# Values of two dilated-attention sections: strided tokens in the matmul, or natural order and a round trip through DRAM

## The chip, the cores and the metric

The program runs on one core of one Trainium2 chip, in one launch. The metric is the device time of that core in microseconds (us). A core has a matrix engine (TensorE, "PE" in the profile, with its weight loads apart as "PEld"), three engines for elementwise work (VectorE "DVE", ScalarE "ACT", GpSimd "POOL"), and queues that issue DMAs (SP, ACT and POOL here). Each engine takes its instructions in the order in which the program lists them.

## What is computed

The reference is a two-layer network of one kind (a convolution with a recurrence, then differential attention) followed by a two-layer network of another. Only the second matters here: each of its two layers mixes tokens by four attentions and then applies a mixture of experts. One of the four is a dilated attention with three branches, each of four heads of width 64:

```python
DIL_BRANCHES = ((128, 1), (512, 4), (2048, 16))
...
q = br(_rope(flat(q), pos))
k = br(_rope(flat(k), pos))
v = br(v)
...
idx = qpos[:, None] - dil * jnp.arange(n_keys)[None, :]
kb = jnp.take(k, idx, axis=1)
vb = jnp.take(v, idx, axis=1)
z = jnp.einsum('bqhd,bqnhd->bhqn', qb, kb) * scale
outs.append(jnp.einsum('bhqn,bqnhd->bhqd', (p / den), vb))
```

There are 512 tokens. In the branches with dilation 4 and 16 a token attends only to tokens of its own residue modulo 4. So the kernel sorts the tokens of these two branches into four classes of 128 tokens (class r holds tokens r, r+4, r+8, ...), and attends within a class.

## The kernel before

Precision is float32, made of pieces: every operand is split into a high part (ACT, L214) and a low part (DVE, L215), and `mm3` (L260 to L265) multiplies three pairs of parts, so three matmuls stand for one. The profile shows them as lines L263, L264 and L265.

Each layer's `mixing` (L1026) runs *sections*. A section projects all tokens to queries and keys (four "columns" j = 0 to 3 of 512 tokens each) and then to values: `value(i, k)` for four groups i of 128 tokens and eight slices k of the input, which is 4 x 8 x 3 = 96 matmuls of 128x256 per section. In a value matmul the tokens `xT` are the stationary operand, the one that a weight load (PEld) puts into the array before each matmul; in a column they are the moving one.

Sections s1 (dilation 4) and s2 (dilation 16) have `classes=True`. Their value matmuls take the tokens of class i at once, by the slice `slice(i, T, 4)` (L1145): every fourth float32 of a row of `xT`. The values land in PSUM in class order and ACT copies them into `r.v` (L1150), a tile with 64 values and a constant 1.0 per head. The queries and keys of these sections are sorted in another way: `rope2` (L1164) computes them in natural order and the split into parts writes them in class order.

`dilated` (L1243) builds the attention of a section: `scores` (L1264; masks L1271, products L1193, row maximum on DVE L1199, exponent on ACT L1204), `transposed` (L1211, copied by ACT L1213), `values` (L1277; products with `r.v`, L1280) and a copy of the result (ACT L1256). `weave` interleaves two lists of steps by their listed costs: d1, the attention of s1, with the columns and values of s2; then d2, the attention of s2, with section s0; then d0 with sb. The values of s1 are not interleaved with anything. The order on PE is fixed by these lists; on the other engines a scheduler sets it when the program is built.

Other parts that the prediction's steps touch:

- `rope2` of column j: ACT and DVE shift halves (L1170, L1171), POOL multiplies by the sine (L1172), DVE multiplies by the cosine (L1173) and adds (L1174), then ACT and DVE split (L214, L215, tile `qd`). L1173 is the last that reads the column's PSUM bank.
- Columns and values share two PSUM banks called `mm` in turn (in s2: columns 0 and 2 and the first pair of value groups use one, columns 1 and 3 and the second pair the other), so a column or a pair of value groups can start only when the `rope2` of the second-last user has read its bank.
- `done` (L998) splits the next weight chunk (tile `wpart`) once the old one has been read, half a chunk at a time.
- `gain` (L481) scales the residual stream (`x`, L486 and L487, on DVE here) and `lend_x` (L1099) copies it to DRAM from the POOL queue (L1103), which lends its tiles to the pool of buffers that `grab` hands out.
- `natural` (L1324) is a round trip through DRAM that exists already: it writes the result of d1 or d2 to DRAM in 128 runs of 4,224 bytes (L1328) and reads it back in token order in 512 runs of 1,056 bytes (L1331), both issued from POOL.

Of the kernel before, what the change touches and what calls it, by code (L numbers as in the profile page):

```python
# [13 lines left out]
F32 = mybir.dt.float32  # L14
# [3 lines left out]
AF = mybir.ActivationFunctionType  # L18
# [5 lines left out]
P = 128  # L24
T = 512
# [104 lines left out]
class _Net:  # L130
# [981 lines left out]
    def section(self, xT, ids, buf, rope=False, classes=False, first=None):  # L1112


        nc = self.nc
        r = SimpleNamespace(steps=[])
        ps = {}

        def column(j, k, toks):
            self.pump()  # L1120
            if (j, k) == (0, 0) and toks.start == 0:
                r.qk = [self.quad_tile(buf, n, [2, T], F32R) for n in range(4)]
            if k == 0 and toks.start == 0:
                ps[j] = self.ps("s" if first and j > 1 else "mm")
            w, o = self.chunk(ids[j // 2]), j % 2 * P
            self.mm3(ps[j][:, toks], [t[:, k, o:o + P] for t in w], [t[:, k, toks] for t in xT], k == 0, k == KD - 1)
            if k < KD - 1 or toks.stop < T:
                return
            if j % 2:
                self.done(ids[j // 2])  # L1130
            parts = r.qk[j][:, 0], r.qk[j][:, 1]
            if rope:
                self.rope2(ps[j], parts, classes, 0.125 if j < 2 else 1.0)
            elif j < 2:
                self.split_scaled(*parts, ps[j], 0.125)
            else:
                self.split(*parts, ps[j])

        def value(i, k):
            self.pump()  # L1140
            if (i, k) == (0, 0):
                r.v = self.vs.pop(0)
            if i % 2 == 0 and k == 0:
                ps["v"] = self.ps("mm")
            toks = slice(i, T, 4) if classes else slice(i * P, (i + 1) * P)  # L1145
            o = i % 2 * 256
            self.mm3(ps["v"][:, o:o + 256], [t[:, k, toks] for t in xT], [t[:, k] for t in self.chunk(ids[2])],
                     k == 0, k == KD - 1)
            if k == KD - 1 and i % 2:
                nc.scalar.activation(r.v[:, i - 1:i + 1, :, 0:64],  # L1150
                                     ps["v"].rearrange("p (i h d) -> p i h d", i=2, h=4), AF.Copy)
                if i == NT - 1:
                    self.done(ids[2])

        for toks in [slice(0, 256), slice(256, T)] if first else [slice(0, T)]:
            for j in range(4):
                if first and toks.start == 0 and 1 <= j <= 2:
                    r.steps.append((0.8, first[j - 1]))
                r.steps += [(0.65, partial(column, j, k, toks)) for k in range(KD)]
        for i in range(NT):  # L1160
            r.steps += [(0.33, partial(value, i, k)) for k in range(KD)]
        return r
# [1121 lines left out]
```

## Time and profile before

| what | value |
|---|---|
| runs (median, lowest to highest) | 2792.08 us, 2788.1 to 2795.29, 3 runs |
| profiled execution: time | 2788.31 us |
| profiled execution: span of the profile | 2786.5 us |
| PE busy | 2664.2 us, 96% of the span |
| PE weight loads | 2232.6 us, 80% |
| DVE, ACT, POOL busy | 60%, 47%, 17% |
| mean granted clock of TensorE | 0.981 of full speed |

A busy PE means that some matmul was in flight; matmuls overlap, so how dense the stream is shows only in the distance between starts. The page gives shares over the whole program; what one stage costs is read from the timeline and the table of stretches.

### The profile page before, as it was taken

How to read it: one execution, taken by the hardware profiler on the slowest of the kernel's cores; microseconds unless marked ns; L12 is line 12 of the kernel's file. 1: busy time of each engine (PE TensorE's matmuls, PEld its weight loads, DVE VectorE, ACT ScalarE, POOL GpSimd, SP SyncE). 2: the span in 40 equal slices, each digit the busy share in tenths (PEclk: the TensorE clock that was granted, in tenths of full speed). 3: DMA queues.
4: the chain of work that ended last, by engine and by line, in shares of the span. 5: the costliest groups of instructions: out<-in, count | busy, mean ns of one | idle time of the engine just before them, and what ended most of it. 6: DMA issues, size and time to landing. Idle time of an engine off the chain costs nothing. (4 is left out here: it accounts for less than half of the span.)

```text
span 2786.5 us, 41347 instructions
## 1 busy us (share of the span) xinstructions
PE 2664.2 (96%) x14504; PEld 2232.6 (80%) x14508; DVE 1678.5 (60%) x2621; ACT 1315.5 (47%) x2076; POOL 469.4 (17%) x430
## 2 busy tenths in 40 slices
PE   8999999999999999999999969999899999799996
PEld 6768888887678888898887768888798877688885
DVE  7785323376866333374445587669764454856897
ACT  5643222255644222244564436558644554246784
POOL 2324000010104000011021141211111120411113
PEclk9999999999999999999999979999999999899998
DMA  6114323213104232322202049979422130279994
GB/s 224 51 46 166 106 84 106 91 71 113 46 31 166 91 98 91 106 78 105 83 31 104 18 178 290 305 220 354 170 91 98 35 111 23 106 256 283 352 366 181
DMA packets 93275, 385.05 MB, mean 138 GB/s; under 512 B 14688, under 2 KB 16480, under 8 KB 76768
## 3 DMA queue, kind: packets, MB, share of 16 engines
q1 hardware_dynamic: 76592, 329.14, 33.3%
q0 software_dynamic: 13408, 47.32, 6.3%
q10 hardware_dynamic: 3024, 5.56, 0.6%
q8 instruction: 118, 1.93, 0.3%
q14 instruction: 133, 1.09, 0.1%
HBM read 349.22 MB, written 32.77 MB: 137 GB/s over the span
## 5 line engine op out<-in xcount | busy, mean ns | idle before, releaser
L215 DVE TENSOR_TENSOR wpart<-raw,wpart 128x1024 fp32r<-128x1024 f32 (+3 forms) x385 | 525.6, 1395 | 315.1 <-ACT wpart L214 298.9
L214 ACT ACTIVATE wpart<-raw 128x1024 fp32r<-128x1024 f32 (+3 forms) x393 | 445.0, 1169 | 363.9 <-PE mm L264 180.5
L263 PE MATMUL mm<-xT,wpart 128*128 128x512 f32 (+1 forms) x1136 | 440.9, 388 | 16.1 <-ACT wpart L214 8.8
L264 PE MATMUL mm<-xT,wpart 128*128 128x512 f32 (+1 forms) x1136 | 428.5, 377 | 1.8 <-DVE xT L215 1.8
L265 PE MATMUL mm<-xT,wpart 128*128 128x512 f32 (+1 forms) x1136 | 427.9, 377 | 0.5 <-DVE wpart L215 0.5
L263 PEld LDWEIGHTS mm<-xT,wpart 128*128 128x128 f32 x1136 | 214.9, 189 | 57.8 <-ACT wpart L214 8.8
L263 PE MATMUL mm<-wpart,xT 128*128 128x256 f32 (+2 forms) x672 | 255.6, 380 | 0.0
L265 PEld LDWEIGHTS mm<-xT,wpart 128*128 128x128 f32 x1136 | 214.8, 189 | 44.3 <-DVE wpart L215 1.0
L264 PEld LDWEIGHTS mm<-xT,wpart 128*128 128x128 f32 x1136 | 215.2, 189 | 41.8 <-DVE xT L215 2.8
L265 PE MATMUL mm<-wpart,xT 128*128 128x256 f32 (+2 forms) x672 | 241.0, 359 | 0.3 <-DVE xT L215 0.2
L264 PE MATMUL mm<-wpart,xT 128*128 128x256 f32 (+2 forms) x672 | 240.2, 357 | 0.0
L349 POOL TENSOR_TENSOR sm<-sm,mhalf 128x4 f32<-128x4 f32 (+2 forms) x74 | 65.4, 884 | 1015.5 <-DVE sm L360 765.6
L264 PE MATMUL mm<-wpart,gT 128*128 128x256 f32 (+1 forms) x544 | 183.7, 338 | 0.0
L265 PE MATMUL mm<-wpart,gT 128*128 128x256 f32 (+1 forms) x544 | 183.2, 337 | 0.0
L263 PE MATMUL mm<-wpart,gT 128*128 128x256 f32 (+1 forms) x544 | 183.1, 337 | 0.0
L263 PEld LDWEIGHTS mm<-wpart,xT 128*128 128x128 f32 x672 | 144.7, 215 | 18.1 <-issue 5.0
L265 PEld LDWEIGHTS mm<-wpart,xT 128*128 128x128 f32 x672 | 144.6, 215 | 14.0 <-DVE xT L930 1.0
L264 PEld LDWEIGHTS mm<-wpart,xT 128*128 128x128 f32 x672 | 145.2, 216 | 10.0 <-issue 1.2
L562 DVE TENSOR_TENSOR silu<-silu,mm 128x512 f32<-128x512 f32 x44 | 30.2, 686 | 200.9 <-PE mm L265 200.9
L215 DVE TENSOR_TENSOR xT<-raw,xT 128x1024 fp32r<-128x1024 f32 x108 | 129.8, 1221 | 17.1 <-ACT xT L214 16.7
L263 PE MATMUL mm<-xT,hT 128*128 128x512 f32 x272 | 114.0, 419 | 1.6 <-ACT xT L214 1.6
L214 ACT ACTIVATE xT<-raw 128x1024 fp32r<-128x1024 f32 x108 | 111.0, 1052 | 5.0 <-DMA raw<-in_w_dram 4.9
(579 smaller groups left out, 5661.0 us busy)
## 6 DMA issues: line engine op xcount, KB each, us to landing
raw<-in_w_dram SPq DMA_DIRECT2D x324, 512.0 KB
raw<-in_gu_dram SPq DMA_DIRECT2D x40, 1024.0 KB
raw<-in_w_in_dram SPq DMA_DIRECT2D x30, 1024.0 KB
raw<-in_down_dram SPq DMA_DIRECT2D x16, 1024.0 KB
raw<-in_o_qk_dram SPq DMA_DIRECT2D x8, 1024.0 KB
raw<-in_w_out_dram SPq DMA_DIRECT2D x8, 1024.0 KB
raw<-in_e_in_dram SPq DMA_DIRECT2D x7, 1024.0 KB
raw<-in_down_dram SPq DMA_DIRECT2D x8, 768.0 KB
```

Of the source, the lines that this page charges most:

```text
L214: ins = self.nc.scalar.activation(hi, x, AF.Copy)
L215: self.last_lo = (eng or self.nc.vector).tensor_sub(lo, x, hi)
L263: mm(out, lhsT=ls[0], rhs=rs[0], start=start, stop=False)
L264: mm(out, lhsT=ls[0], rhs=rs[1], start=False, stop=False)
L265: mm(out, lhsT=ls[1], rhs=rs[0], start=False, stop=stop)
L349: self.last_rsqrt = self.nc.gpsimd.tensor_tensor(v, v, self.half[:, :n], op=ALU.pow)
L562: nc.vector.tensor_mul(s, s, ps[2 * j + 1])
```

## The change

In sections with `classes=True` the value matmuls take the tokens in natural order, 128 neighbours at a time, as the other sections do. Since the values then lie by token and not by class, they go through DRAM: ACT copies a pair of value groups (128x512) into a buffer, POOL's queue writes it to a DRAM tile `vperm` of 512 x 256 floats, and after the second pair a third DMA reads `vperm` back into `r.v`, partition j from tokens 4j to 4j+3, as 2,048 runs of 256 bytes (a head's 64 values; the constant beside them stays). Per section that adds two DMAs of 256 KB out and one of 512 KB in, all on POOL's queue, and two buffers; the ACT copy stays, with another destination. There are four such sections, s1 and s2 in each of two layers.

```diff
             if (i, k) == (0, 0):
                 r.v = self.vs.pop(0)
+                if classes:
+                    r.vd = self.dram.tile([T, 256], F32, name=self.uid("vperm"))
             if i % 2 == 0 and k == 0:
                 ps["v"] = self.ps("mm")
-            toks = slice(i, T, 4) if classes else slice(i * P, (i + 1) * P)
+            toks = slice(i * P, (i + 1) * P)
...
             if k == KD - 1 and i % 2:
-                nc.scalar.activation(r.v[:, i - 1:i + 1, :, 0:64],
-                                     ps["v"].rearrange("p (i h d) -> p i h d", i=2, h=4), AF.Copy)
+                if classes:
+
+                    v = self.grab()
+                    nc.scalar.activation(v, ps["v"], AF.Copy)
+                    nc.gpsimd.dma_start(r.vd[(i - 1) * P:(i + 1) * P].rearrange("(i p) c -> p i c", i=2),
+                                        v.rearrange("p (i c) -> p i c", i=2))
+                    self.drop(v)
+                else:
+                    nc.scalar.activation(r.v[:, i - 1:i + 1, :, 0:64],
+                                         ps["v"].rearrange("p (i h d) -> p i h d", i=2, h=4), AF.Copy)
                 if i == NT - 1:
                     self.done(ids[2])
+                    if classes:
+                        nc.gpsimd.dma_start(r.v[:, :, :, 0:64], r.vd.rearrange("(j r) (h d) -> j r h d", r=4, h=4))
```

Lines behind the change move by 12, so L1172 of before is L1184 of after, L1103 stays.

POOL in the first of the two layers, around the values of s1: `xk` are the copies of the residual stream x to DRAM, the multiplications are those of `rope2`. Before:

```order
L1172 TENSOR_TENSOR mx_8296<-mx_8296,cf 128x512
L1172 TENSOR_TENSOR mx_8298<-mx_8298,cf 128x512
L1103 DMA xk_8733<-x_76 128x1024
L1103 DMA xk_8733<-x_77 128x1024
L1172 TENSOR_TENSOR mx_8302<-mx_8302,cf 128x512
```

And after:

```order
L1184 TENSOR_TENSOR mx_8298<-mx_8298,cf 128x512
L1156 DMA vperm_8620<-mx_8300 128x2x256
L1156 DMA vperm_8620<-mx_8301 128x2x256
L1103 DMA xk_8737<-x_76 128x1024
L1165 DMA mx_8307<-vperm_8620 128x16x64
L1103 DMA xk_8737<-x_77 128x1024
L1184 TENSOR_TENSOR mx_8293<-mx_8293,cf 128x512
```

The read back (L1165) stands behind the third copy of x, and before the fourth and the first `rope2` of s2.

POOL in the same layer, around the values of s2, where `perm` is the round trip of d1's result. Before:

```order
L1172 TENSOR_TENSOR x_76<-x_76,cf 128x512
L1328 DMA perm_9119<-mx_8303 128x1056
L1331 DMA mx_8304<-perm_9119 128x4x264
L1172 TENSOR_TENSOR mx_8296<-mx_8296,cf 128x512
L1172 TENSOR_TENSOR x_76<-x_76,cf 128x512
```

And after:

```order
L1184 TENSOR_TENSOR x_76<-x_76,cf 128x512
L1156 DMA vperm_8995<-mx_8294 128x2x256
L1340 DMA perm_9127<-mx_8303 128x1056
L1156 DMA vperm_8995<-mx_8302 128x2x256
L1343 DMA mx_8304<-perm_9127 128x4x264
L1165 DMA mx_8308<-vperm_8995 128x16x64
L1184 TENSOR_TENSOR mx_8292<-mx_8292,cf 128x512
```

The two round trips are interleaved, and the read of the values stands behind both reads' waits, ahead of the first `rope2` of s0.

ACT keeps its order: the copy of a pair stands where L1150 stood. Around the values of s1 it is, after:

```order
L1182 ACTIVATE mx_8298<-s_8456 32x512
L1155 ACTIVATE mx_8300<-mm_8621 128x512
L214 ACTIVATE qd_8330<-mx_8297 128x128x4
L214 ACTIVATE qd_8331<-mx_8299 128x128x4
L214 ACTIVATE wpart_87<-raw_82 128x1024
L1155 ACTIVATE mx_8301<-mm_8675 128x512
L214 ACTIVATE wpart_87<-raw_82 128x1024
```

Here `qd_8330` and `qd_8331` are the splits of columns 2 and 3 and `wpart_87` the next chunk for the values of s2; nothing moved. On PE, DVE and ACT no instruction changes its place among the others anywhere in the mixing. On SP one load of output weights (L996) and two small loads (L1490) trade places later in the mixing. Since each of the four sections takes two more buffers from `grab`, the buffers that later steps get are others than before.

## Rows read from the trace of the kernel before

**Rows 1.** The page, part 1: busy time and share of each engine.
```profile
PE 2664.2 (96%) x14504; PEld 2232.6 (80%) x14508; DVE 1678.5 (60%) x2621; ACT 1315.5 (47%) x2076; POOL 469.4 (17%) x430
```

**Rows 2.** Stretches: start:end, length, us busy of PE, PEld, DVE, ACT, POOL, clock, DMA.
```profile
1236.00:1258.60 22.60, 22.60 (x100) 22.56 (x100) 19.90 (x22) 8.29 (x10) 4.97 (x4) 1.00 0.33 116
1258.60:1313.00 54.40, 54.40 (x294) 48.69 (x294) 26.38 (x32) 24.80 (x44) 6.38 (x7) 1.00 0.23 78
1313.00:1356.40 43.40, 43.35 (x293) 37.57 (x294) 22.98 (x31) 22.67 (x45) 6.46 (x6) 1.00 0.25 85
...
2041.40:2095.80 54.40, 54.40 (x293) 48.69 (x292) 25.84 (x32) 24.80 (x44) 5.84 (x6) 1.00 0.23 84
```

**Rows 3.** Groups by shape: weight loads of s1's values (strided tokens), 1236.0 to 1258.6.
```profile
L264 PEld LDWEIGHTS mm<-wpart,xT 128*128 128x128 f32 x32 | 10.6, 330 | 0.0
```

**Rows 4.** The same view for s0's values (neighbouring tokens), 1341.6 to 1356.4.
```profile
L264 PEld LDWEIGHTS mm<-wpart,xT 128*128 128x128 f32 x32 | 6.0, 188 | 0.0
```

**Rows 5.** Timeline, PE: start, duration, engine, line; s1's first value, d1's steps, s2's values.
```profile
1236.17 0.40 PE L263 MATMUL mm<-wpart,xT 128*128 128x256 f32 x1
...
1258.58 0.61 PE L1271 MATMUL s<-cb,identb 128*128 128x512 bf16 x2
1259.11 1.55 PE L1193 MATMUL s<-qd,qd 64*128 64x128 f32 x24
...
1268.40 0.60 PE L1211 MATMUL t<-cf,mx 128*128 128x128 f32 x4
...
1279.81 1.00 PE L1280 MATMUL o<-mx,mx 128*128 128x65 f32 x8
...
1281.40 0.39 PE L263 MATMUL mm<-xT,wpart 128*128 128x512 f32 x1
...
1287.35 0.48 PE L263 MATMUL mm<-wpart,xT 128*128 128x256 f32 x1
```

**Rows 6.** Timeline, PE, s0's values: two starts, 15 matmuls apart.
```profile
1342.08 0.28 PE L265 MATMUL mm<-wpart,xT 128*128 128x256 f32 x1
...
1343.84 0.28 PE L265 MATMUL mm<-wpart,xT 128*128 128x256 f32 x1
```

**Rows 7.** Timeline, DVE, s1's values to s2's first column; idle before, its releaser in brackets.
```profile
1249.22 1.08 DVE L215 TENSOR_TENSOR qd<-mx,qd 128x512 fp32r<-128x512 f32 x1 [0.75 <-ACT qd L214]
...
1257.06 1.23 DVE L215 TENSOR_TENSOR wpart<-raw,wpart 128x1024 fp32r<-128x1024 f32 x1 [1.60 <-ACT wpart L214]
...
1260.35 1.23 DVE L215 TENSOR_TENSOR wpart<-raw,wpart 128x1024 fp32r<-128x1024 f32 x1 [0.93 <-ACT wpart L214]
1261.49 1.28 DVE L1199 TENSOR_REDUCE sm<-s 128x4 f32<-128x512 f32 x2
1267.12 0.68 DVE L1171 TENSOR_SCALAR mx<-mm 32x512 f32<-32x512 f32 x1 [4.35 <-ACT mx L1170]
```

**Rows 8.** Timeline, ACT, same stretch: copy of the first pair, d1's first exponents.
```profile
1247.57 0.60 ACT L1150 ACTIVATE mx<-mm 128x512 f32<-128x512 f32 x1 [4.38 <-PE mm L265]
...
1262.21 2.17 ACT L1204 ACTIVATE mx<-s,sm 128x128 f32<-128x128 f32 x8 [1.90 <-DVE sm L1199]
```

**Rows 9.** Timeline, DVE: last read of the PSUM banks of s2's columns 1, 2, 3.
```profile
1279.98 0.69 DVE L1173 SCALAR_TENSOR_TENSOR mx<-mm,cf 128x512 f32<-128x512 f32 x1
1286.48 0.69 DVE L1173 SCALAR_TENSOR_TENSOR x<-mm,cf 128x512 f32<-128x512 f32 x1
1294.43 0.69 DVE L1173 SCALAR_TENSOR_TENSOR x<-mm,cf 128x512 f32<-128x512 f32 x1
```

**Rows 10.** Line L1328, the write of `natural`: time from issue to landing.
```profile
DMA to landing us min/median/max: 3.0/3.0/3.0
```

**Rows 11.** Line L1331, the read of `natural`: its issue, and its time to landing.
```profile
L1331 POOL DMA_DIRECT2D mx<-perm x4: 766/779/793, 1312.9 to 2141.0; - x4
...
DMA to landing us min/median/max: 4.1/4.1/4.1
```

**Rows 12.** The page, part 3: packets, MB and share of 16 engines of POOL's queue.
```profile
q0 software_dynamic: 13408, 47.32, 6.3%
```

## Prediction
> **What bounds the kernel now.** I read the page first: PE is busy for 96% of the span and its weight loads for 80%, while POOL, which gets the added work, has 17% [rows 1]. Then I read the stretch that the change touches, as a table of stages [rows 2]: in s1's values, in d1 with s2 and in d2 with s0, PE is busy nearly all the time at the full granted clock (1.00, the 2.4 GHz level). So a microsecond taken out of the matmul stream there is a microsecond of the program, unless another engine is late once PE is faster. The table has a hint of what can be taken out: d1 with s2 and d2 with s0 run the same steps with the same number of matmuls (294 and 293), but the first takes 54.40 us and the second 43.40 us, and weight loads are busy for 48.69 and 37.57 us. The one difference on PE is that s2 takes strided tokens in its values and s0 neighbours.
>
> The groups by shape confirm it. A weight load of the same shape from the same tile takes 330 ns with every fourth token [rows 3] and 188 ns with neighbours [rows 4]. What counts is the distance between starts: s1's 96 value matmuls run from 1236.17 to the start of d1 at 1258.58 [rows 5], 22.41 us or 233.4 ns each; s0's are 1.76 us for 15, or 117.3 ns each [rows 6].
>
> **The gain on PE.** Per section 96 x (233.4 - 117.3) ns = 11.1 us, the same as the 11.0 us between the two stages. The second layer repeats it (54.40 us for d1 with s2 there too [rows 2]). Four sections give 44.6 us, if nothing else is late.
>
> The Trainium skill has a rule that speaks against this. "SBUF — State Buffer", section "Door 1: The DMA port swizzle", says that SBUF has lines of 16 bytes, that every step to a new line costs, and that one can therefore stride for free over up to four float32. Read as it stands, a stride of exactly four would be free and the sum would be nought. The rows decide: at that stride the load takes 330 instead of 188 ns, so the part of the rule on new lines agrees and the allowance does not.
>
> **What becomes late, s1.** Nothing is interleaved with s1's values, and they now cover the rope of columns 2 and 3. They would end at 1236.17 + 96 x 0.1173 = 1247.4 instead of 1258.58, and d1's first products need column 2's split, whose low part DVE finished at 1249.22 + 1.08 = 1250.3 [rows 7]. Of that, 0.75 us [rows 7] is idle time behind ACT, whose split stood behind the copy of the first value pair; that copy waited for PE until 1247.57 [rows 8] and can now start some 4 us earlier, when ACT comes to it. So column 2 is split at about 1249.55. The masks of d1 take 0.53 us ahead of the products (1258.58 to 1259.11 [rows 5]); the products start at 1249.6 instead of 1248.0: **1.6 us lost**.
>
> Next is d1's first transposition. In before it came 9.3 us after the products' start, at 1268.40 [rows 5]; its input was ready long before, since DVE reached the maximum at 1261.49 [rows 7] and ACT the exponents at 1262.21 [rows 8]. Ahead of that maximum DVE has a fixed list: two splits, two gains, two halves of a weight chunk. In before it idled 0.75, 1.60 and 0.93 us in it [rows 7], and without these 3.3 us and with some hand-over the maximum comes at about 1258.05. It can't come earlier, since DVE was busy for 19.90 us of the 22.60 of this stretch [rows 2]. Exponents then start at about 1258.8 and the first head's four need half of 2.17 us [rows 8], so the transposition starts at 1260.0, where PE alone would be at 1258.9: **1.05 us lost**. PE is now 8.4 us ahead of before, but the DVE and ACT chain only 3.4 us by its first step; it catches up to some 5.5 us (DVE next idled 4.35 us [rows 7] behind ACT, which waited for a column on PE, and half of that goes) and then stays 2.9 us behind PE.
>
> **What becomes late, s2.** That chain frees the PSUM banks. Column 3 of s2 started at 1281.40 in before, 0.7 us behind the last read of column 1 (1279.98 + 0.69), and the values at 1287.35 [rows 5], 0.2 us behind column 2's read (1286.48 + 0.69 [rows 9]). With a chain 2.9 us behind PE, these two margins are gone and about **2.8 us are lost** before the values start at 1281.75. The second pair of values then waits for column 3's read, in before 7.8 us after the values' start (1294.43 + 0.69 [rows 9]). One step of that chain waits for a copy of d1's result behind value matmuls and comes about 0.7 us sooner, so 7.0 us, where PE would be there after 48 x 0.1173 us plus 0.3 of a transposition = 5.9: **1.1 us lost**. In s0, whose splits are not strided and cost DVE and ACT less, the same place has no wait that I can see (43.35 of 43.40 us busy [rows 2]).
>
> Per layer 1.6 + 1.05 + 2.8 + 1.1 = 6.55 us of 22.2 go back, 15.65 remain; for two layers **31.3 us**.
>
> **What the round trip costs.** ACT has the same number of copies of the same size: nothing. POOL gets three issues per section. The write to DRAM has a model in `natural`: 3.0 us from issue to landing for 528 KB in 128 runs [rows 10]. The read has none with runs of 256 bytes. Its nearest row is `natural`'s read, 0.78 us of issue and 4.1 us to landing for 512 runs of 1,056 bytes [rows 11]. The low end is that row itself, 4.1 us, since the bytes are about the same; the high end is four times it, 16.4 us, in proportion to the runs. Between them, the 384 runs that this row has more than the write cost 1.1 us, so another 1,536 make 4.4 us: I take 8.5 us. For the issue I take the high end, 3.1 us, since it costs nothing below either.
>
> In s1 the second copy is behind column 3's split and half a weight chunk on ACT and ends at about 1253.1; the write lands at 1256.2, and POOL issues the read then. The third copy of x ahead of it waits for a gain that ends at about 1253.6, so it costs nothing. The values land at 1264.7 (1260.3 to 1272.6). d1's first value product stood 20.7 us behind its products' start (1279.81 [rows 5]); by the losses above it comes at 1271.4. So 6.7 us are spare, and even the high end costs only 1.2 us. Behind the waiting POOL stand the last copy of x and the first sine of s2, due at about 1263.7; POOL is free at about 1259.9. In s2 both round trips interleave: the second copy ends 0.9 us after the start of d2, the write lands 3.0 us later, the read between 8.0 and 20.3 us after d2's start, and d2's first value product stands 21.2 us behind it, as in d1 (1258.58 to 1279.81 [rows 5]). Nothing is lost; the first sine of s0 is due 10.8 us behind d2's start and POOL free after 7.0. At no cost I put as well the trade on SP and the other buffers: each is reused only tens of microseconds later.
>
> In "DMA: Bandwidth & Descriptors", section "Specifications", the Trainium skill wants at least 512 bytes per run for full rate and says that shorter ones are read, modified and written. That speaks for the high end here; no run shows it at 256 bytes yet. By it the sum would lose up to 2.4 us, 1.2 per layer.
>
> **Sum.** The profiled execution took 2788.31 us for a span of 2786.5; 2788.31 - 31.3 = 2757.0. Its own time is 3.8 us under the median of the runs, inside their spread of 7.2 us, so the range gets that much at its upper end.
>
> **The rivals.** *Full gain*: ACT and DVE lose no time, for instance because DVE's operations run faster beside a less busy POOL; for it, d2 with s0 runs dense with neighbours; against it, DVE has 88% of s1's values [rows 2] and its stretch is to be halved. Time 2788.3 - 44.6 = 2743.7; chance 0.17. *Half gain*: the lagging chain costs twice what I found, since every step of it waits for the one before and I walked only the longest; 2 x 6.55 per layer leaves 18.2 us, 2770; for it, the 88% of DVE; against it, DVE idled 4.35 us right behind [rows 7]; chance 0.14. *Slower*, one mechanism: the read of `r.v` is late. POOL's queue took 13,408 packets in 6.3% of 16 engines' span [rows 12], that is 0.21 us each; if each run of 256 bytes costs as much, 128 runs per engine make 26.8 us, with the 3.0 us of a landing about 30. PE, which takes its instructions in order, would stand still at d1's first value product for 30 - 15.2 = 14.8 us and at d2's for 12.5 us. With 3.75 us of the other losses (the 2.8 vanish in the first wait) that is 31 against 22.2 per layer: 17.6 us slower, 2806. It decides from a landing of 25.5 us on. Against it: `natural`'s read of 512 runs, 32 per engine, landed in 4.1 us, which 0.21 us each would not allow. Chance 0.04. *It does not do what it says*: the stride is not the cause of the 330 ns but something else of these sections; then PE keeps its pace and the time stays within 1 us, 2788. Against it: same line, tile, shape and clock in both groups [rows 3, 4]. Chance 0.03. The allowance of the Trainium skill's "SBUF — State Buffer" would have the same result.
>
> **How the numbers follow.** My forecast, a gain of 25 to 38 us (2750 to 2763), has a chance of 0.62; with the others 1.00. The predicted time is 2757. The range takes in full gain and half gain, 2743 to 2772, and leaves out between 0.1 and 0.2. About 0.3% (8.4 us) is what a measurement of this kernel can tell from no change. Faster by more: 0.62 + 0.17 + 0.13 = 0.92; within: 0.04 (the last rival and a part of half gain); slower: 0.04.
>
> **What would show it.** Weight loads of s1's and s2's values at 188 ns with starts 117 ns apart: right on the gain. From s1's first value to d2's start 76.8 us in before; 61.2 after by the forecast, 54.6 at full gain. A gap on PE of 1.6 us at d1's products, 1 us at its first transposition, and waits on DVE's L1185 at column 3 and the values: right on the losses. A wait of the value products (L1292) for a DMA would show the late read, and a landing of the read (L1165) over 15 us that my 8.5 is wrong. What would make the forecast wrong altogether is a chain on DVE that lags longer than to the end of s2, or weight loads that stay at 330 ns.

## The result

The changed kernel takes 2757.57 us (median, 2755.84 to 2759.37), the kernel before beside it 2790.09 us (2787.06 to 2795.29): a ratio of 0.9878 with a 95% interval of 0.9866 to 0.9890. The forecast was 2757.0 us. The profiled execution took 2755.84 us for a span of 2754.1, 32.5 us less than the 2788.31 us of the execution that the rows ahead of this section come from.

In the rows of the changed kernel L1183 to L1185 are the rope's L1171 to L1173 of before, L1292 multiplies with the values, L1155 copies a pair of values, L1156 writes it to DRAM and L1165 reads it back. In some kernels of the experiments these lines stand up to 15 further down: L1186, L1187 and L1200 in VectorE's rows below are this L1185.

One group of weight loads by shape, in s1's values (line, engine, operation, tiles, shape and count; busy time, mean ns; idle before). It answers [rows 3]:

```profile
L264 PEld LDWEIGHTS mm<-wpart,xT 128*128 128x128 f32 x32 | 6.0, 188 | 0.0
```

The groups of the other two lines have 187 and 188 ns, and in s2's values all three have 188: the loads are at the time of neighbours. The rows of TensorE in order of time (start, duration, engine, line, operation, tiles; in brackets the idle time before and who ended it), from s1's first value to d2's masks. They answer [rows 5]; this execution is 2.79 us behind that of before when the values begin. Three dots stand for rows left out.

```profile
1238.96 0.28 PE L263 MATMUL mm<-wpart,xT 128*128 128x256 f32 x1
...
1250.27 0.60 PE L1283 MATMUL s<-cb,identb 128*128 128x512 bf16 x2
1250.80 0.33 PE L1205 MATMUL s<-qd,qd 64*128 64x128 f32 x2
1252.36 1.45 PE L1205 MATMUL s<-qd,qd 64*128 64x128 f32 x22 [1.23 <-DVE qd L215]
...
1263.08 0.60 PE L1223 MATMUL t<-cf,mx 128*128 128x128 f32 x4
...
1274.49 1.00 PE L1292 MATMUL o<-mx,mx 128*128 128x65 f32 x8
...
1278.06 0.61 PE L263 MATMUL mm<-xT,wpart 128*128 128x512 f32 x1 [1.82 <-DVE mx L1185]
...
1300.07 0.60 PE L1283 MATMUL s<-cb,identb 128*128 128x512 bf16 x2
```

In the kernel before, d2 starts here:

```profile
1312.98 0.60 PE L1271 MATMUL s<-cb,identb 128*128 128x512 bf16 x2
```

The values now take 1250.27 - 1238.96 = 11.31 us instead of 22.41, and from the first value to d2's start it is 1300.07 - 1238.96 = 61.11 us instead of 1312.98 - 1236.17 = 76.81. That distance is the measure in all that follows; I call it **the stage**. In the second layer it went from 76.81 to 61.03 us. Two waits have appeared that [rows 5] do not have, 1.23 us at d1's products and 1.82 us at column 3 of s2. A third thing shows only in the table of stretches (start:end, length, then busy time of PE, its weight loads, DVE, ACT and POOL with their counts, then PE's granted clock, DMA share and GB/s):

```profile
1238.80:1250.30 11.50, 11.50 (x100) 11.46 (x100) 11.24 (x14) 6.23 (x8) 4.45 (x4) 1.00 0.27 91
1250.30:1252.36 2.06, 0.83 (x6) 0.27 (x4) 2.06 (x3) 0.01 (x1) 0.71 (x1) 1.00 0.37 127
1252.36:1254.20 1.84, 1.84 (x24) 1.72 (x25) 1.76 (x3) 1.26 (x2) 0.00 (x0) 1.00 0.05 13
1254.20:1258.20 4.00, 4.00 (x13) 3.09 (x12) 4.00 (x4) 2.17 (x3) 1.30 (x2) 0.57 0.77 258
1258.20:1276.00 17.80, 17.80 (x103) 14.19 (x101) 11.68 (x16) 10.50 (x25) 3.02 (x3) 1.00 0.48 163
1276.00:1278.00 2.00, 0.24 (x2) 0.00 (x0) 1.85 (x3) 0.73 (x2) 0.66 (x1) 1.00 0.43 61
1278.00:1281.80 3.80, 3.74 (x10) 2.95 (x11) 1.95 (x3) 1.69 (x2) 0.61 (x1) 0.55 0.58 244
1281.80:1300.10 18.30, 18.30 (x145) 17.54 (x144) 10.44 (x13) 9.88 (x14) 3.92 (x4) 1.00 0.23 78
```

Behind the two pauses the granted clock is 0.57 and 0.55 on average over 4.00 and 3.80 us, that is for the most part at 0.50, the 1.2 GHz level; in the kernel before it was 1.00 throughout [rows 2]. And VectorE is busy for 19.06 us of the 19.40 up to 1258.20.

### The profile page after: what moved, and what is told of

The parts are those of the page before. It is cut to its first block, busy times and chain, and to the rows that moved or that the text cites. A ratio compares the mean times of both kernels' runs of the same rounds, so it can differ in the third digit from the quotient of the medians.

```text
span 2754.1 us, 41408 instructions
## 1 busy us (share of the span) xinstructions
PE 2625.0 (95%) x14508; PEld 2189.1 (79%) x14508; DVE 1676.2 (61%) x2621; ACT 1315.0 (48%) x2076; POOL 478.5 (17%) x442
## 5 line engine op out<-in xcount | busy, mean ns | idle before, releaser
L263 PE MATMUL mm<-wpart,xT 128*128 128x256 f32 (+2 forms) x672 | 241.0, 359 | 0.0
L265 PE MATMUL mm<-wpart,xT 128*128 128x256 f32 (+2 forms) x672 | 226.8, 338 | 0.3 <-DVE xT L215 0.2
L264 PE MATMUL mm<-wpart,xT 128*128 128x256 f32 (+2 forms) x672 | 225.5, 336 | 0.0
L263 PEld LDWEIGHTS mm<-wpart,xT 128*128 128x128 f32 x672 | 127.0, 189 | 18.6 <-issue 5.4
L215 DVE TENSOR_TENSOR xT<-raw,xT 128x1024 fp32r<-128x1024 f32 x108 | 129.8, 1221 | 15.8 <-ACT xT L214 15.3
L265 PEld LDWEIGHTS mm<-wpart,xT 128*128 128x128 f32 x672 | 126.6, 188 | 14.5 <-DVE xT L215 1.2
L264 PEld LDWEIGHTS mm<-wpart,xT 128*128 128x128 f32 x672 | 127.1, 189 | 10.1 <-issue 1.2
```

Source lines behind the costliest of these rows:

```text
L215: self.last_lo = (eng or self.nc.vector).tensor_sub(lo, x, hi)
L263: mm(out, lhsT=ls[0], rhs=rs[0], start=start, stop=False)
L264: mm(out, lhsT=ls[0], rhs=rs[1], start=False, stop=False)
L265: mm(out, lhsT=ls[1], rhs=rs[0], start=False, stop=stop)
```

## The experiments

Theory: the gain comes from the weight loads. Of the 22.2 us per layer 6.5 are lost, because VectorE's list of operations does not shorten with the loads; the loss shows partly as pauses of TensorE and partly as a lower clock behind them. The round trip is hidden. The rivals stand in the expectations. Three kernels compute other values, which can send tokens to other experts behind the stage; their whole time is no measure ("not comparable"), and only the stage is read. All stages in one table (us, first and second layer; ratio to the kernel before, from runs on the same chip, with its interval):

| kernel | stage | median us | ratio |
|---|---|---|---|
| before | 76.81, 76.81 | 2790.1 | 1 |
| changed | 61.11, 61.03 | 2757.6 | 0.9878 (0.9866 to 0.9890) |
| changed, run again | 61.16, 61.09 | 2758.4 | 0.9883 (0.9866 to 0.9899) |
| no round trip | 60.52, 61.67 | not comparable | |
| round trip alone | 76.84, 76.84 | 2794.2 | 1.0001 (0.9991 to 1.0010) |
| first section alone | 72.33, 72.27 | 2784.3 | 0.9972 (0.9963 to 0.9982) |
| second section alone | 66.10, 66.10 | 2772.0 | 0.9931 (0.9913 to 0.9949) |
| strides of two and three | 66.84, 66.75 | not comparable | |
| no gain and bias | 55.69, 55.73 | not comparable | |
| half of them on GpSimd | 58.70, 58.37 | 2766.6 | 0.9911 (0.9894 to 0.9927) |
| pauses filled | 60.81, 60.71 | 2759.4 | 0.9886 (0.9868 to 0.9903) |
| half of them later | 55.69, 56.02 | 2750.2 | 0.9855 (0.9841 to 0.9868) |
| half of them later, run again | 55.78, 56.04 | 2751.3 | 0.9851 (0.9834 to 0.9867) |
| read three times | 71.20, 65.51 | 2795.5 | 1.0010 (0.9997 to 1.0023) |

### Is it the loads, and is the trip free?

The first kernel has no round trip, and the values stay in the wrong order. The edit stands at three places, the buffer in DRAM, the copy with the write, and the read:

```diff
-                if classes:
+                if False:
```

> The changed kernel without the round trip: the values of both strided sections are computed for neighbouring tokens and copied straight into the tile that the products read, with no write to DRAM, no read and no GpSimd DMA instruction; the reordering of the tokens is left out, everything else stays. Theory (the trip is wholly hidden, the gain is the weight loads alone): 2757 us, within 2 us of the changed kernel, and the same two waits of TensorE per layer. Rival (the trip costs something that the waits do not name, by DMA traffic or the GpSimd queue): 5 us or more under the changed kernel, at most 2744, the time of the full gain.

Its whole time, 2811.3 us, was a miss of the expectation: I had not thought of the routing. The busy line of its page (first) and that of the changed kernel differ by 320 matmuls, nearly all of them in the experts' layers:

```profile
PE 2679.0 (95%) x14828; PEld 2235.9 (80%) x14832; DVE 1698.8 (60%) x2651; ACT 1337.5 (48%) x2109; POOL 478.7 (17%) x436
```

```profile
PE 2625.0 (95%) x14508; PEld 2189.1 (79%) x14508; DVE 1676.2 (61%) x2621; ACT 1315.0 (48%) x2076; POOL 478.5 (17%) x442
```

The stage itself has no routing in it: 60.52 and 61.67 us, on average 61.10 where the changed kernel has 61.07. The two layers differ by 0.6 us to either side, so the trip costs nothing there that could be told from that.

The second keeps the strided loads and adds the round trip alone:

```diff
-            toks = slice(i * P, (i + 1) * P)
+            toks = slice(i, T, 4) if classes else slice(i * P, (i + 1) * P)
...
-                    nc.gpsimd.dma_start(r.vd[(i - 1) * P:(i + 1) * P].rearrange("(i p) c -> p i c", i=2),
+                    nc.gpsimd.dma_start(r.vd.rearrange("(j r) c -> j r c", r=4)[:, i - 1:i + 1],
```

> The round trip alone: the weight loads of the values keep the stride of four tokens as before the change, and the values, already in the order of the classes, are still written to DRAM (each row to its token's place) and read back with the same transfer as in the changed kernel. Theory (the gain is the loads' alone and the trip is hidden): 2790 us, no different from before within 3 us, with loads of 330 ns. Rival (the trip costs time of its own): 2795 us or more. Rival (the gain came from somewhere else than the stride, for instance from the copies into a plain buffer): 2775 or less.

Ratio 1.0001, stage 76.84: as the theory said. Neither the trip nor the copies into a plain buffer give or take anything by themselves.

The third asks what a load pays for its stride; it is the kernel before, with strides of two and three tokens in place of four:

```diff
-            toks = slice(i, T, 4) if classes else slice(i * P, (i + 1) * P)
+            toks = slice(i * P, (i + 1) * P)
+            if classes:
+                toks = slice(i, i + 382, 3) if buf else slice(i // 2 * 256 + i % 2, i // 2 * 256 + i % 2 + 255, 2)
```

> The kernel before the change with other strides in the weight loads of the values: the first strided section takes 128 tokens two apart, the second 128 tokens three apart, instead of four; the values then belong to other tokens than they should, and what they do to the routing behind the stage makes the whole time no measure. What is read is the duration and the spacing of the loads. Theory (a load pays for every token that it steps over): between 188 and 330 ns in equal parts, 235 ns at a stride of two and 283 ns at three. Rival (the price comes whole with any stride over one): 330 ns at both. Rival (strides under four tokens, 16 bytes, are free): 188 ns at both.

The groups of loads in s1's values (stride two) and in s2's (stride three):

```profile
L264 PEld LDWEIGHTS mm<-wpart,xT 128*128 128x128 f32 x32 | 6.4, 199 | 0.0
...
L264 PEld LDWEIGHTS mm<-wpart,xT 128*128 128x128 f32 x31 | 8.2, 264 | 0.0
```

199 and 264 ns: neither the theory nor a rival had these. A stride of two costs 11 ns more than neighbours, three 76, four 142. The distance between starts tells more (the granted clock is 1.00 in both stretches). s1's 96 values take 1249.53 - 1238.01 = 11.52 us, 120 ns each, and two consecutive starts in s2 are 175 ns apart on average (1293.09 to 1294.14 for six). At strides of three and four, 175 and 233.4 ns are 58 ns for each element of the stride. Two of these would be 117 ns, no more than the 118 ns at which products of 256 columns follow each other with neighbours, so a stride of two costs next to nothing. The Trainium skill's "SBUF — State Buffer", section "Door 1: The DMA port swizzle", lets one stride for free over up to four float32; for these loads it holds up to two.

### Where the rest of the gain goes

Two kernels have the change in one section alone (`buf == 0` for the first, 1 for the second; `trip` stands in the place of `classes` at the buffer, the write and the read too):

```diff
+        trip = classes and buf == 0
...
-            toks = slice(i * P, (i + 1) * P)
+            toks = slice(i, T, 4) if classes and not trip else slice(i * P, (i + 1) * P)
```

> The change in the first strided section alone, in both layers; the second keeps the strided loads and the direct copy. Its values end 11.1 us earlier, and the first branch's scores and the second section's columns start that much earlier against VectorE's list. Theory (the 6.5 us lost in a layer are waits, and clock after the waits, that this earlier start causes): a gain of 11.1 - 6.5 = 4.6 us per layer, 9.3 in all, 2781 us, with the same two waits (1.2 and 1.8 us in the first layer) and the clock at its lower level for about 4 us behind each. Rival (the loss comes with the second section): 22 us, 2768. Rival (an equal share from each section): 16 us, 2774.

> The change in the second strided section alone; the first keeps the strided loads and the direct copy, so that the first branch's scores start when they did before the change. Theory (the loss comes from the first section's earlier end): the second section's 11.1 us per layer come out nearly whole, since VectorE and ScalarE stand as before; 20 to 22 us in all, 2768 to 2770 us, and no wait of TensorE for VectorE at the scores or the columns, all stretches at a granted clock of 1.00. Rival (equal shares): 16 us, 2774. Rival (the loss comes with the second section): 9 us, 2781.

The stage gets shorter by 4.48 and 4.54 us with the first section alone (4.6 expected) and by 10.71 with the second (10 to 11), in sum 15.2 of the 15.7 of the whole change. In the whole time, 0.9972 is 7.8 us (5 to 10) and 0.9931 is 19.3 (14 to 24). So the loss belongs to the first section, as the theory had it: its values end 11.1 us earlier, and 6.6 of these are lost again. The waits of TensorE in the first layer's stage (who waits, for whom; total, times, longest) with the second alone:

```profile
PE mm L263 <- DVE x L1186: 0.2, 1, 0.2
```

and in the second layer with the first alone:

```profile
PE mm L263 <- DVE mx L1186: 2.5, 1, 2.5
PE t L1224 <- ACT mx L1217: 1.4, 1, 1.4
```

In the first layer with the first alone the waits are not the two expected, 1.2 and 1.8 us, but 1.22 at the products, 0.27 at the transposition and 2.47 at column 3, and the clock falls behind the last alone; the stage is the same, 72.33 us.

Is it VectorE's list? The gain and bias of the layer norm (`gain`) stand in it, eight operations of 1.2 us in each layer. The next kernel leaves them out:

```diff
...
-                gain()
                 self.lend_x()
```

> The changed kernel without the gain and bias of the layer norm on the four rows of x in the mixing stage (eight VectorE operations of 1.2 us per layer are left out, so that the routing behind the stage differs and the whole time is no measure). What is read is the time from the first section's first value to the second branch's first scores, 61.1 us in the changed kernel, 54.6 with no loss. Theory (VectorE's list, with these eight operations in it, makes TensorE wait, and the clock falls behind the waits): no wait over 0.5 us and 54.6 to 56 us. Rival (the waits come from ScalarE's or GpSimd's part of the chain): 59 us or more, with the wait at the second section's column still there.

55.69 us; only the two value pairs wait, 0.25 us each, and the clock is at 1.00 through the whole stage. Taking eight operations from VectorE gives back 5.4 of the 6.5 us, with ScalarE's and GpSimd's steps of the rope in place.

That leaves the clock. In the first layer pauses and clock seem to share the loss: 1.23 + 1.82 us of waits, and 4.00 x 0.43 + 3.80 x 0.45 = 3.4 us of clock. To part them, TensorE gets something to do in the pauses: products that nobody reads, into a PSUM bank that a later result overwrites. `fill` is five in d1's first unit and nought elsewhere:

```diff
+    def busy(self, n):
...
+        for _ in range(n):
+            self.nc.tensor.matmul(ps, lhsT=self.xT[0][:, 0, :P], rhs=self.xT[0][:, 0], start=True, stop=True)
...
+                if n == 1 and fill and cs == place[0][0]:
+                    self.busy(fill)
...
+            if classes and buf and (j, k) == (3, 0):
+                self.busy(7)
```

> The changed kernel with TensorE kept busy where it waits: five products of 128x512 into an idle bank of PSUM ahead of the scores' second third in the first unit, and seven ahead of column 3 of the second section, in both layers (0.23 us each; their result is read by nobody). They shorten no wait, they only fill it. Theory (the fall of the granted clock to half is what the pause brings about, and costs 1.7 us each of three times): the clock stays at 1.00 in all these stretches, and 5 us are gained, 2752 us. Rival (the clock falls for another reason): the clock falls all the same, 2757 us, or up to 2760 where the products do not fit into the waits.

The stretches of this kernel over the same steps (columns as above; the fourth and fifth are column 3's pause and what follows):

```profile
1247.90:1251.46 3.56, 3.56 (x34) 2.47 (x32) 3.56 (x4) 0.88 (x2) 0.79 (x2) 1.00 0.24 81
1251.46:1256.00 4.54, 4.54 (x22) 3.68 (x21) 4.47 (x5) 2.63 (x4) 1.30 (x2) 1.00 0.71 233
1256.00:1273.00 17.00, 16.75 (x96) 12.94 (x95) 10.87 (x16) 9.80 (x24) 3.01 (x3) 1.00 0.54 171
1273.19:1275.81 2.62, 1.76 (x8) 1.16 (x7) 2.41 (x3) 1.27 (x3) 0.72 (x1) 1.00 0.23 38
1275.81:1280.00 4.19, 4.19 (x18) 3.42 (x19) 2.37 (x3) 1.73 (x2) 0.55 (x1) 1.00 0.56 227
```

and TensorE's rows at column 3:

```profile
1273.19 1.76 PE L1202 MATMUL idle<-xT 128*128 128x512 f32 x7
1275.81 0.47 PE L263 MATMUL mm<-xT,wpart 128*128 128x512 f32 x1 [0.86 <-DVE mx L1187]
```

Half of the theory held: the clock stays at 1.00 when the pauses are filled, so the pauses are what it falls behind. The other half fell: the stage is 0.3 us shorter in each layer, not 3.4 in the first and 1.7 in the second, and the time is no different from the changed kernel's. With the clock up, TensorE reaches column 3 earlier and only waits longer there: 1273.19 to 1275.81 is 2.62 us, filled or idle, against 1.82 in the changed kernel.

The first layer's stage in three legs shows why. They are cut at two of VectorE's rows: the start of the first row maximum, and the end of the L1185 that frees the bank for column 3. In the changed kernel, with the pauses filled, and with half of the gains later (below), the second cut is:

```profile
1277.22 0.69 DVE L1185 SCALAR_TENSOR_TENSOR mx<-mm,cf 128x512 f32<-128x512 f32 x1
...
1274.97 0.69 DVE L1187 SCALAR_TENSOR_TENSOR mx<-mm,cf 128x512 f32<-128x512 f32 x1
...
1271.10 0.69 DVE L1200 SCALAR_TENSOR_TENSOR mx<-mm,cf 128x512 f32<-128x512 f32 x1
```

| kernel (us) | first value to maximum | to the end of L1185 | to d2's start |
|---|---|---|---|
| before [rows 7, 9] | 25.32 | 19.18 | 32.31 |
| changed | 21.85 | 17.10 | 22.16 |
| changed, run again | 21.86 | 17.14 | 22.16 |
| first section alone | 21.86 | 17.12 | 33.35 |
| pauses filled | 21.92 | 17.12 | 21.77 |
| no gain and bias | 17.01 | 17.10 | 21.58 |
| half of them later | 17.03 | 17.10 | 21.56 |

With the loads at 188 ns in the first section the clock moves neither of the first two legs, and only the gains shorten the first. In the first VectorE works through its list almost without a break; in the second VectorE and ScalarE wait for each other in turns (in the changed kernel VectorE's waits there are 2.26, 0.66, 2.10 and 0.27 us for ScalarE and 0.69 for GpSimd). A slow TensorE hurts little where other engines set the pace.

### Relieving VectorE

The first try puts half of the gain and bias on GpSimd, which is idle there. The loop behind this line runs over the two halves:

```diff
-            eng = self.nc.gpsimd if on_pool else self.nc.vector
+            halves = ((self.nc.vector, self.xs[:2], self.ln_end), (self.nc.gpsimd, self.xs[2:], self.last_rsqrt))
...
```

> The changed kernel with half of the gain and bias moved: the rows x2 and x3 (four operations per layer) are done by GpSimd ahead of its rope products, x0 and x1 stay on VectorE; nothing is left out. VectorE then reaches the split of column 2 some 1.2 us earlier and the first maximum 4.7 us earlier. Theory (VectorE's list causes the waits): the waits at the first products and at the second section's column vanish in both layers with the clock's fall behind them, 6 us per layer, 2745 us. Rival (waits come from elsewhere, or GpSimd's operations of 2.9 us delay its rope products by as much): 2757 us or more.

It is slower than the changed kernel by about 9 us: the rival's number, but for a reason that it had not named. The stage is 2.4 and 2.7 us shorter; the loss lies ahead of it. VectorE's rows, then GpSimd's:

```profile
1228.68 6.74 DVE L489 TENSOR_TENSOR x<-x,qd 128x1024 f32<-128x1024 f32 x2
1235.35 4.55 DVE L490 TENSOR_TENSOR x<-x,qd 128x1024 f32<-128x1024 f32 x2
```

```profile
1224.45 6.56 POOL L489 TENSOR_TENSOR x<-x,qd 128x1024 f32<-128x1024 f32 x2 [8.35 <-DVE xT L215]
1230.97 6.71 POOL L490 TENSOR_TENSOR x<-x,qd 128x1024 f32<-128x1024 f32 x2
```

Beside GpSimd's, VectorE's own two multiplications take 6.74 us instead of 2.35, and its rope of column 0 comes so late that s1's first value waits 5.60 us for a bank (6.28 in the second layer). The Trainium skill's "SBUF — State Buffer", section "SBUF: two separate sides", says that an operation of VectorE with two inputs in SBUF and one of GpSimd that reads SBUF exclude each other, and that the one that comes second is blocked until the first is done; the 3.37 us of a multiplication that takes 1.2 alone agree.

The second try leaves all of them on VectorE and does half of them later: x2 and x3 where all four stood, x0 and x1 behind the split of column 3. Their rows of gain and bias wait in two tiles that are idle until then:

```diff
...
-                gain()
-                self.lend_x()
+                gain((self.outs[3], self.outs[2]), (2, 3))
+                self.lend_x((2, 3))
...
+                def rest():
+                    gain(None, (0, 1))
+                    self.lend_rows((0, 1))
+
+                s2.steps.insert(32, (0.0, rest))
```

> The changed kernel with half of the gain and bias moved on VectorE itself: x2 and x3 (four operations per layer) stay ahead of the rope, x0 and x1 are done behind the split of the second section's column 3, with their rows of gain and bias in two tiles that are idle until then; GpSimd is not used and nothing is left out. VectorE reaches the split of column 2 1.2 us earlier and the first maximum 4.8 us earlier. Theory (VectorE's list ahead of the first maximum makes the waits): the waits at the first products and at column 3 vanish with the clock's fall behind them, first value to the second branch's first scores 56 us as without any gain, 5 us less in each layer, 2747 to 2749 us. Rival (the whole work on VectorE counts, wherever it stands, since the stage is bound by its sum): 61 us and 2757. Rival (the later operations hold up the second branch's first maximum): 2752 or more, with a new wait at the second branch's transposition.

VectorE's rows of gain and bias in the first layer, of which the upper two are x2's and x3's:

```profile
1226.44 2.35 DVE L492 TENSOR_TENSOR x<-x,mx 128x1024 f32<-128x1024 f32 x2
1228.71 2.35 DVE L493 TENSOR_TENSOR x<-x,mx 128x1024 f32<-128x1024 f32 x2
...
1289.33 2.35 DVE L492 TENSOR_TENSOR x<-x,mx 128x1024 f32<-128x1024 f32 x2
1291.61 2.35 DVE L493 TENSOR_TENSOR x<-x,mx 128x1024 f32<-128x1024 f32 x2
```

and its first row maximum, 17.03 us behind the first value at 1237.66, 4.8 us earlier than in the changed kernel:

```profile
1254.69 1.28 DVE L1226 TENSOR_REDUCE sm<-s 128x4 f32<-128x512 f32 x2
```

Stage 55.69 and 56.02 us, the waits in the first layer down to this:

```profile
PE mm L263 <- DVE x L1200: 0.5, 2, 0.3
```

With all of the gain and bias done, the stage is as short as without any. So it is not the sum of VectorE's work that counts but what stands ahead of the first maximum. The whole time, 2750.2 us, is a little over the 2747 to 2749 expected. Both kernels were run once more on one chip:

> The changed kernel as it is, beside the version with half of the gain and bias behind column 3 (the next run), on the same chip, to set the one against the other. Theory: 2757 us, a gain of 32 to 33 us on the kernel before.

> The changed kernel with x0's and x1's gain and bias behind the split of the second section's column 3, beside the changed kernel on the same chip. Theory (the stage is 5.4 and 5.0 us shorter in the two layers, and all of it comes out): 10 us under the changed kernel, 2747. Rival (the later operations cost part of it in the stages behind): 7 us under it, 2750.

2758.35 us (2753.18 to 2760.72) and 2751.32 (2746.66 to 2752.66): 7.0 us less, the number of the rival, and 0.9851 (0.9834 to 0.9867) of the kernel before. In the profiles the stages are 5.38 and 5.05 us shorter, 10.4 together. Whether the missing 3 us are lost in the stages behind, as the rival has it, or lie in the spread of the runs is open: from the second layer's d2 to the end two executions of this version took 690.8 and 696.9 us.

### How much slack the trip has

The last kernel issues each read of the values three times:

```diff
-                        nc.gpsimd.dma_start(r.v[:, :, :, 0:64], r.vd.rearrange("(j r) (h d) -> j r h d", r=4, h=4))
+                        for _ in range(3):
+                            nc.gpsimd.dma_start(r.v[:, :, :, 0:64], r.vd.rearrange("(j r) (h d) -> j r h d", r=4, h=4))
```

> The changed kernel with each read of the values from DRAM issued three times in a row into the same tile (the same bytes each time), so that the last lands later by two more issues of 1.2 us and two more transfers of 512 KB. In the changed kernel the DMA engines are at rest from 1270.0 us, and the first product with the values starts at 1274.5. Theory (there are 4 us and more of slack, each further read takes 1.2 to 3.0 us): the values land between 1272.4 and 1276.0, no wait or one of at most 1.5 us per layer in the first section, 2757 to 2760 us. Rival (the read stands at its limit): a wait of 5 us and more at the products with the values in both layers, 2768 us or more.

A miss: 38 us slower than the changed kernel. In its profile 14.6 us of that lie in the two stages and 19.7 between d2's start and d0's, where the reads of s2's values are. GpSimd's rows in the first stage show why:

```profile
1257.16 1.18 POOL L1166 DMA_DIRECT2D mx<-vperm  x1 [3.09 <-DMA vperm<-mx]
...
1266.03 1.17 POOL L1166 DMA_DIRECT2D mx<-vperm  x1 [7.14 <-DMA mx<-vperm]
1271.81 1.16 POOL L1166 DMA_DIRECT2D mx<-vperm  x1 [4.62 <-DMA mx<-vperm]
1272.98 1.27 POOL L1185 TENSOR_TENSOR mx<-mx,cf 128x512 f32<-128x512 f32 x1
```

I had let the reads queue one behind the other; but they write the same tile, so each is issued only when the one before has landed, and GpSimd stands still meanwhile with the sine of s2 behind it. What was meant as 1.2 to 3.0 us per read was 5.6 to 5.8. That the time rises says therefore little of the trip itself, but the rows measure what the changed kernel's trace does not print: the first read lands 1266.03 - 1257.16 = 8.9 us after its issue, the second after 5.8. TensorE's first product with the values:

```profile
1277.44 1.94 PE L1293 MATMUL o<-mx,mx 128*128 128x65 f32 x8 [5.94 <-DMA mx<-vperm]
```

It would have come at 1277.44 - 5.94 = 1271.5, so one read, landed at 1266.03, has 5.5 us to spare.

## Point by point

**The gain.** Loads of 188 ns and starts 117.8 ns apart (11.31 us for 96) are what this step forecast. The second section alone gives 10.7 of the 11.1 us forecast for a section. The 22.2 us of a layer are nearly all there when VectorE is relieved (76.81 - 55.69 = 21.1, with 0.5 us of waits).

**The loss.** 76.81 - 61.11 = 15.7 us remain in the first layer and 15.8 in the second; 15.65 were forecast. The chain of VectorE and ScalarE behind it was right in its size and place: on this execution's time, 2.79 us later, column 2's split, the maximum and the first value product were to come at 1252.3, 1260.84 and 1274.2.

```profile
1251.29 1.02 DVE L215 TENSOR_TENSOR qd<-mx,qd 128x512 fp32r<-128x512 f32 x1
...
1260.81 1.28 DVE L1211 TENSOR_REDUCE sm<-s 128x4 f32<-128x512 f32 x2
```

They came at 1252.31, 1260.81 and 1274.49. The chain was to be 3.4 us ahead of before at the maximum and to catch up to 5.5; by the first two legs it is 25.32 - 21.85 = 3.47 us ahead and then 3.47 + 19.18 - 17.10 = 5.55.

How TensorE spends its time was not right. Forecast were four pauses, 1.6, 1.05, 2.8 and 1.1 us. In the first layer there are two, 1.23 and 1.82, with the clock at half behind them; in the second 1.41 at the transposition and 2.46 at column 3, with the clock at half behind the last alone. The second pair of values waits in neither. Another execution of the same kernel has 1.24, 0.26 and 2.47 in its first layer, with the clock at half behind the last alone and the same stage, 61.16 us. The prediction left the clock out. This did no harm because its sum was made along the chain of VectorE and ScalarE, and what TensorE does while it is ahead of that chain does not count: with the pauses filled and the clock at 1.00 the stage is only 0.3 us shorter.

**What was not named.** The prediction took VectorE's list ahead of the maximum as fixed ("two splits, two gains, two halves of a weight chunk"). The change does leave it as it is, but the gains can stand elsewhere, and that is worth 5 us per layer. The list itself was misread: from column 2's split to the maximum VectorE's rows of before have two splits, an addition of the rope, three operations of the gains and three halves of a weight chunk. This did not touch the sum, which took only the idle times out of that stretch.

**The round trip.** Hidden, as forecast. The read's landing was taken at 8.5 us and is 8.9, the slack at 6.7 us and is 5.5 (both measured with three reads). The write's landing was taken at 3.0 us; from its issue at 1255.73 to the read's at 1260.10 it is 4.4. The issue of the read was put at its upper end, 3.1 us, and takes 1.17. The queue's packets bear on the price of 256-byte runs (queue, packets, MB, share of 16 engines). The changed kernel has, and the one with three reads:

```profile
q0 software_dynamic: 14624, 51.52, 6.9%
```

```profile
q0 software_dynamic: 15776, 55.71, 7.3%
```

Eight more reads are 1,152 packets, 144 for each, of 3.6 KB on average: the 2,048 runs of 256 bytes are not a packet each. The rival of the late read, whose 30 us rested on a packet per run, falls with that. The Trainium skill's "DMA: Bandwidth & Descriptors", section "Specifications", asks for at least 512 bytes for full rate. The read is indeed slower than one with runs four times as long, 8.9 us for the first and 5.8 for the second against 4.1 [rows 11], but far from the 16.4 of the high end.

**The other rivals.** Full gain would be 54.6 us for the stage: it is 55.7 once the list is relieved, but not in this kernel. Half gain would be 67.7 us, against 61.11. That the stride is not the cause of the 330 ns is excluded by the loads of 188, 199 and 264 ns at strides of one, two and three.

## What to carry to other kernels

When a step gets faster, another engine may become the one that sets the pace. Then sum along that engine's chain and not over the pauses of the one that got faster: between two executions of one kernel the pauses changed, and the stage did not (61.11 and 61.16 us). See what stands in the slower engine's list only by habit: four operations moved some 60 us later brought back 5 of the 6.5 us lost in a layer. And a transposition of the data through DRAM can be cheaper than a strided operand, where there is time between the last result and its first use (here 13.3 us, 4.4 for the write and 8.9 for the read, of 18.8).

## What the runs showed of the hardware

- In the changed kernel pauses of TensorE of 1.23, 1.82 and 2.46 us were each followed by about 4 us in which the granted clock fell to 0.50, the 1.2 GHz level. With the pauses filled by products that nobody reads, the clock stayed at 1.00. It didn't fall behind every pause: behind the 1.41 us at the second layer's transposition, and behind 1.24 and 1.22 us at d1's products in the changed kernel run again and with the first section alone, it was 1.00. In the first layer's stage the falls cost 0.3 us of the 3.4 that the stretches suggest.
- A weight load of 128x128 fp32 takes 188, 199, 264 and 330 ns at strides of one, two, three and four elements. The products behind such loads start 118, 120, 175 and 233 ns apart, at three and four 58 ns per element of the stride.
- The same multiplication of 128x1024 on VectorE took 1.2 us alone and 3.4 beside one on GpSimd.
- Eight reads of 512 KB with runs of 256 bytes took 1,152 packets of 3.6 KB on average. With three reads in a row the first of them in the first stage landed 8.9 us after its issue, the next after 5.8.
